# Attention of a hybrid layer: two query blocks score into one two-bank tile, and weighted values, transposes and scores of neighbouring steps form one run on TensorE

## The chip, the cores and the metric

The kernel runs on one core of a Trainium2 chip. The metric is device time in microseconds (us) of one execution; the time of a kernel is the median of its runs. The engines are TensorE (PE, with PEld for its weight loads), VectorE (DVE), ScalarE (ACT), GpSimd (POOL) and SyncE (SP). Each engine takes its own instructions in a fixed order and waits on semaphores.

## The reference

One inference step of one layer: a combined input projection of RMSNorm(x) feeds a convolution branch and a dilated sliding-window attention; both are gated, projected and added; a gated feed-forward with a short convolution follows. 1024 prompt tokens and 8 sample tokens (1032 columns) run together. The change concerns the attention of the prompt:

```python
D_MODEL, SEQ, HEAD_DIM, HEADS_PER_GROUP = 1024, 1024, 64, 4
GROUPS = ((128, 1), (512, 4), (2048, 16))          # window, dilation
...
    s = jnp.einsum('brnqhd,brnkhd->brnhqk', qb, kb).astype(jnp.float32)
    ...
    s = jnp.where(valid[None, None, :, None], s, NEG)
    mx = jnp.max(s, axis=-1, keepdims=True)
    p = jnp.exp(s - mx)
    den = jnp.sum(p, axis=-1, keepdims=True)
    o = jnp.einsum('brnhqk,brnkhd->brnqhd', p, vb.astype(jnp.float32))
    o = o / jnp.swapaxes(den[..., 0], -1, -2)[..., None]
```

After permuting the tokens by the dilation, every group has eight blocks of 128 queries for each head. A block sees its own 128 keys and, where one exists, the 128 before it.

## The kernel before, in words

Attention is done in six units, one for each group g and pair of heads p; unit b = 2g + p. A unit (`attention_unit`, L570) writes three projection jobs, q, k and v, by `in_jobs`: each makes three banks of 344 columns, 24 matmuls to a bank (`product`, matmul at L215; three passes of split operands over eight blocks of depth). ACT evacuates each bank (L553), DVE applies the rotary embedding to q and k (`rope`, L538 to L549). After each bank `mm_blocks` calls `pump` (L125), which takes the next item or items of queues: `later` (one item, and one more for each `LD` = 9 that wait), `second`, `third`, and `taps`, the depthwise convolution (`conv_wide`, L494, one tap of some 1000 columns on DVE at a time, L502). So attention's steps and the taps are written between the banks of projections of the units that follow; after unit 5 the gate projections ga and gb are the cover. A scheduler then gives each engine its fixed order, following what is written, the buffers and its own idea of times; `after` adds an order between two instructions.

The items of a unit are `values` (L589: eight transposes of v, two banks), ten of `step` (L644), the samples' scores, and `store`. `step(t)` weighs block t − 2, turns block t − 1 and scores block t:

- `scores(i)` (L599): for each head a matmul (L612) of 64 rows, 128 queries by 128 or 256 keys, into a one-bank tile of tag "s" (two of them); then a DVE reduction (L613) that adds the mask, writes `sm` and gives the maximum; one negation `nm` (L617) for both heads; two exponentials on ACT (L620) that write `pr` and the denominators. Of the 48 blocks 22 have 256 keys and 26 have 128.
- `turn(i)` (L623): transposes of `pr` on PE (L629; two or four) into a bank of tag "t", evacuated by ACT as `pk` (L631).
- `weigh(i)` (L633): two or four matmuls with the values (L639), into a bank of tag "o", evacuated by ACT into `ot` (L642).

`sm`, `pr` and `pk` have two buffers each. The eight banks of PSUM are given by tag: mm 4, s 2, t 1, o 1. `combine` (L696) later weighs the groups, `layer_norm` (L778) belongs to the convolution branch; both use banks of the same tags.

## Time and profile before

| | before |
|---|---|
| time, median of three runs | 1666.64 us (1660.62 to 1666.67) |
| profiled execution | 1664.54 us, span 1662.8 us |
| PE busy | 1622.7 us, 98% |
| DVE busy | 1125.7 us, 68% |
| ACT busy | 608.1 us, 37% |
| POOL busy | 178.4 us, 11% |
| mean granted clock of PE | 0.993 |

The profile is one execution, taken on the chip. Its span runs from the first to the last instruction. Busy is the union of an engine's instructions; matmuls are pipelined, so that a row lasts longer than the step to the next one. A windows view cuts the span into stretches and gives busy time for each engine; the timeline lists instructions by start; the chain of waits follows the last work back to what released it. The attention stretch is 229 to 570 us.

### The profile page before, as it was taken

Reading aid. Unit: us, or ns where it says so; the run is one execution under the profiler, and the core shown is the slowest. Engines: PE = TensorE matmul, PEld = TensorE weight load, DVE = VectorE, ACT = ScalarE, POOL = GpSimd, SP = SyncE. Lnnn points to the kernel's source line nnn. Section 1 sums busy time; section 2 is a strip of 40 time slices with the busy share of each in tenths; the row PEclk is TensorE's granted clock in tenths of the full one; section 3 lists DMA queues with packets and bytes.
Section 4 is the critical chain, followed back from the end, with each engine's and each line's share of the span. In section 5 each row is a group of like instructions: output and inputs, shape, how many; then the busy total and the mean of one; then the engine's idle time right before and its main releaser. Section 6 shows DMA issues by size and latency. Waiting matters only on the chain.

```text
span 1662.8 us, 26829 instructions
## 1 busy us (share of the span) xinstructions
PE 1622.7 (98%) x11044; PEld 1576.3 (95%) x11044; DVE 1125.7 (68%) x1747; ACT 608.1 (37%) x1079; POOL 178.4 (11%) x269
## 2 busy tenths in 40 slices
PE   8999999999999999999999989999999999999997
PEld 7999998898899999999999989999999998999997
DVE  5889998798986996764435786666666666324246
ACT  6411123344434223452223454444444444221023
POOL 0111011011102102130001001111111110000002
PEclk9999999999999999999999999999999999999999
DMA  8544332232325457893553135655655557752102
GB/s 291 187 129 125 95 118 81 83 94 80 116 92 191 137 171 247 225 355 127 184 195 117 49 115 153 178 153 153 178 153 153 153 128 271 286 197 83 48 26 102
DMA packets 86986, 250.19 MB, mean 150 GB/s; under 512 B 10128, under 2 KB 31664, under 8 KB 86864
## 3 DMA queue, kind: packets, MB, share of 16 engines
q1 hardware_dynamic: 57984, 157.85, 28.6%
q0 software_dynamic: 28880, 90.64, 18.9%
q8 instruction: 86, 1.41, 0.3%
q14 instruction: 36, 0.29, 0.1%
HBM read 201.11 MB, written 92.46 MB: 177 GB/s over the span
## 4 chain that ended last, share of the span: by engine, by line
PE 85%; DMA 7%; DVE 3%; ACT 2%; issue 2%; SPq 0%; POOL 0%; DVEq 0%; POOLq 0%; ACTq 0%
PE dn L215 13%; PE qb L1077 9%; PE ga L215 6%; PE oa L215 5%; PE gb L215 5%; PE xo L215 5%; PE v L215 4%; PE k L215 4%; PE q L215 4%; PE qc L1077 4%; PE al L215 4%; DMA sa<-w_ups 3%; PE ag L215 3%; PE first L215 3%; PE qa L1077 2%; PE s L612 2%
## 5 line engine op out<-in xcount | busy, mean ns | idle before, releaser
L502 DVE SCALAR_TENSOR_TENSOR ca<-cu,c_w_dw,ca 128x1019 f32<-128x1019 f32 (+22 forms) x240 | 300.3, 1268 | 1.7
L215 PE MATMUL dn<-gl,hi_wd 128*128 128x344 f32 x456 | 147.5, 323 | 2.6 <-DVE gl L68 2.6
L215 PE MATMUL dn<-gh,hi_wd 128*128 128x344 f32 x456 | 147.0, 323 | 1.2 <-ACT gh L68 1.2
L215 PE MATMUL dn<-gh,lo_wd 128*128 128x344 f32 x456 | 146.8, 322 | 0.0
L934 DVE TENSOR_TENSOR xs<-dn,xs 128x1032 f32<-128x1032 f32 x26 | 32.0, 1232 | 123.0 <-PE dn L215 115.9
L1057 DVE TENSOR_TENSOR sb<-sa,raw_ra 128x512 f32<-128x512 f32 x20 | 13.8, 692 | 114.7 <-DMA sa<-w_ups 112.9
L215 PEld LDWEIGHTS dn<-gl,hi_wd 128*128 128x128 f32 x456 | 86.6, 190 | 4.4 <-DVE gl L68 4.4
L215 PEld LDWEIGHTS dn<-gh,hi_wd 128*128 128x128 f32 x456 | 86.5, 190 | 1.9 <-ACT gh L68 1.9
L215 PEld LDWEIGHTS dn<-gh,lo_wd 128*128 128x128 f32 x456 | 86.5, 190 | 0.0
L68 ACT ACTIVATE hi_wd<-raw_wd 128x896 fp32r<-128x896 f32 (+1 forms) x24 | 23.7, 987 | 140.7 <-PE dn L215 139.0
L1077 PE MATMUL qb<-t,hi_wc 128*128 128x258 f32 x320 | 60.4, 289 | 7.4 <-ACT s L1128 7.4
L215 PE MATMUL xo<-mh,hi_wo 128*128 128x344 f32 x192 | 62.3, 325 | 3.3 <-DVE xr L960 3.3
L215 PE MATMUL ga<-hh,lo_ga 128*128 128x344 f32 x192 | 62.5, 325 | 0.0
L215 PE MATMUL ga<-hh,hi_ga 128*128 128x344 f32 x192 | 62.4, 325 | 0.0
L215 PE MATMUL ga<-hl,hi_ga 128*128 128x344 f32 x192 | 62.3, 325 | 0.0
L215 PE MATMUL xo<-ml,hi_wo 128*128 128x344 f32 x192 | 62.1, 324 | 0.0
L215 PE MATMUL gb<-hl,hi_gb 128*128 128x344 f32 x192 | 62.0, 323 | 0.0
L215 PE MATMUL xo<-mh,lo_wo 128*128 128x344 f32 x192 | 61.9, 322 | 0.0
L215 PE MATMUL gb<-hh,lo_gb 128*128 128x344 f32 x192 | 61.8, 322 | 0.0
L215 PE MATMUL oa<-sl,hi_wco 128*128 128x344 f32 x192 | 61.5, 320 | 0.0
L215 PE MATMUL oa<-sh,lo_wco 128*128 128x344 f32 x192 | 61.5, 320 | 0.0
L215 PE MATMUL gb<-hh,hi_gb 128*128 128x344 f32 x192 | 61.1, 318 | 0.0
(820 smaller groups left out, 5429.4 us busy)
## 6 DMA issues: line engine op xcount, KB each, us to landing
o_k<-cache_k SPq DMA_DIRECT2D x16, 1023.5 KB, 7.4
o_v<-cache_v SPq DMA_DIRECT2D x16, 1023.5 KB, 7.7
g<-g_dram SPq DMA_DIRECT2D x22, 516.0 KB, 8.2
sa<-w_ups SPq DMA_DIRECT2D x20, 512.0 KB, 3.6
sa<-w_ups POOLq DMA_DIRECT2D x20, 512.0 KB, 5.7
raw_ra<-w_ups SPq DMA_DIRECT2D x20, 512.0 KB, 3.6
raw_wd<-w_down SPq DMA_DIRECT2D x16, 448.0 KB, 3.2
hi_wd<-w_ups POOLq DMA_DIRECT2D x20, 256.0 KB, 3.5
```

The source lines that it names most:

```text
L68: ins = op(*args, **kwargs)
L215: ins = nc.tensor.matmul(ps[:, :m], wk, xk, start=(k == 0 and i == 0), stop=(k == n - 1 and i == 2))
L502: after(anchor[0], nc.vector.scalar_tensor_tensor(acc[:, d:SEQ], u[:, :SEQ - d], w[:, 30 - d:31 - d], acc[:, d:SEQ], ALU.mult, ALU.add))
L612: nc.tensor.matmul(sps[:, :nk], q[hs, i * P:(i + 1) * P], k[hs, k0:k0 + nk], start=True, stop=True)
L934: nc.vector.tensor_tensor(out=v3(t), in0=ps, in1=v3(t), op=ALU.add)
L1057: nc.vector.tensor_tensor(out=s2, in0=s1, in1=ra[:, 512:], op=ALU.add)
L1077: nc.tensor.matmul(ps[:, s, :SUB], wk, xk, start=(first and k == 0 and i == 0), stop=(k == 3 and i == 2), skip_group_check=True)
```

## The change

The score tile of tag "s" becomes one tile of two banks, one bank for each head, with two query blocks side by side in a bank. A step now handles two blocks: a unit has six steps, in which step t weighs double block t − 2, turns t − 1 and scores t. Four score matmuls follow each other, then four reductions, one negation of four maxima, and four exponentials. The second transposed block of a step goes into a bank of tag "mm". Weighted values of both blocks, and the samples' products, share one "o" bank and one evacuation.

`run` and `ready` bind a step on PE. `after(run[0], ...)` holds transposes behind the weighted values of the step and scores behind the transposes. `ready(exps[t], ...)` is a semaphore dependence: the transposes of double block t, and the weighted values of t − 1 that stand before them, wait for the last exponential of t. So the three pieces stand as one run with no projection between. `values` and the transposes in `combine` use the two-bank tile and one evacuation each; the small sums of `layer_norm` take banks of three tags and lose two yields inside loops.

```diff
-PSA = {"mm": 4, "s": 2, "t": 1, "o": 1}
+PSA = {"mm": 4, "s": 1, "t": 1, "o": 1}
...
+    def two_banks(name):
+        return psb[0].tile([P, 2, 512], F32, tag="s", name=name, bufs=1)
...
+    def ready(first, then):
+        tc.add_manual_dep(
+            then.ins, first.ins.name,
+            mybir.DependencyInfo(mybir.DependencyClass.Sync, mybir.DependencyReason.DATA),
+            reason="together",
+        )
...
         def values():
...
+            ps = two_banks(f"vtr{b}")
+            for i in range(8):
+                nc.tensor.transpose(ps[:, i // 4, i % 4 * P:(i % 4 + 1) * P], vt[:, i * P:(i + 1) * P], ident)
+            nc.scalar.activation(v, ps.rearrange("p h (i c) -> p (h i) c", c=P), AF.Copy)
...
+        probs, turned, exps, extra, run = {}, {}, {}, [], [None]
+        def scores(t):
+            sps = two_banks(f"s{b}{t}").rearrange("p h (i k) -> p h i k", i=2)
+            for i in (2 * t, 2 * t + 1):
+                nk, k0, _ = keys(i)
+                for h in range(2):
+                    hs = slice(h * HALF, (h + 1) * HALF)
+                    after(run[0], nc.tensor.matmul(sps[:, h, i % 2, :nk], q[hs, i * P:(i + 1) * P], k[hs, k0:k0 + nk],
+                                                   start=True, stop=True))
+            nm = small.tile([P, 2, 2], F32, tag="nm", name=f"nm{b}{t}")
...
+                for h in range(2):
+                    nc.vector.tensor_tensor_reduce(
+                        out=sms[i][:, h, :nk], in0=sps[:, h, i % 2, :nk], in1=mask, scale=1.0, scalar=-3e38,
+                        op0=ALU.add, op1=ALU.max, accum_out=mx[:, i % 2, h:h + 1])
             anchor[0] = nc.vector.tensor_scalar(nm, mx, -1.0, None, ALU.mult)
...
+                for h in range(2):
+                    exps[t] = nc.scalar.activation(
+                        probs[i][:, h, :nk], sms[i][:, h, :nk], AF.Exp, bias=nm[:, i % 2, h:h + 1],
+                        accum_out=ot[:, i, 2 * HALF + 2 + h:2 * HALF + 3 + h])
+
+        def turn(t):
+            for i, tag in ((2 * t, "t"), (2 * t + 1, "mm")):
...
+                        ins = nc.tensor.transpose(tps[:, o:o + P], probs[i][:, h, kb * P:(kb + 1) * P], ident)
+                        ready(exps[t], ins)
+                        after(run[0], ins)
+                run[0] = ins
...
+        def weigh(t):
+            ops = bank(f"o{b}{t}", "o")
...
+                        run[0] = nc.tensor.matmul(ops[:, c:c + HALF], turned[i][:, o:o + P],
+                                                  v[:, k0 // P + kb, h * HALF:(h + 1) * HALF],
+                                                  start=(kb == 0), stop=(kb == nk // P - 1))
+                        if t + 1 in exps:
+                            ready(exps[t + 1], run[0])
+            for products in extra:
+                products(ops[:2 * NS, 2 * P:3 * P + 1])
+            extra.clear()
+            nc.scalar.activation(ot[:, 2 * t:2 * t + 2, :2 * HALF], ops[:, :2 * P].rearrange("p (i c) -> p i c", i=2),
+                                 AF.Copy)
 
         def step(t):
+
             if 0 <= t - 2:
                 weigh(t - 2)
-            if 0 <= t - 1 < 8:
+            if 0 <= t - 1 < 4:
                 turn(t - 1)
-            if t < 8:
+            if t < 4:
                 scores(t)
...
-        for t in range(10):
+        for t in range(6):
             later.append(lambda t=t: step(t))
-            if t == 1:
-                later.append(lambda: later.insert(3, sample_scores()))
+            if t == 0:
+                later.append(lambda: later.insert(3, lambda products=sample_scores(): extra.append(products)))
...
+        ps = two_banks(f"otr{p}")
+        for i in range(8):
+            nc.tensor.transpose(ps[:, i // 4, i % 4 * P:(i % 4 + 1) * P], os_[0][:, i, :], ident)
+        split(ps.rearrange("p a b -> p (a b)"), oT_h[:, :SEQ], oT_l[:, :SEQ])
+        yield
...
+            ps = bank(f"lm{c}", "sto"[c])
             nc.tensor.matmul(ps[:, :CW], onesm, c_sum[:, cs(c)], start=True, stop=True)
             nc.scalar.activation(mub[:, cs(c)], ps[:, :CW], AF.Copy, scale=1.0 / DM)
-            yield
+        yield
```

The order of the built programs shows what this does at three places. Names end in a running number; s51 is step 1 of unit 5, in the kernel before s521 is block 2, head 1. In the kernel after, the matmul of `product` is L226, scores L618, transposes L647, weighted values L662, reductions L628, the negation L631, taps L513, exponentials L636.

PE, unit 5, before, at block 2:

```order
L612 MATMUL s520_5014<-k5r_4604,q5r_4424 128x128
L612 MATMUL s521_5017<-k5r_4604,q5r_4424 128x128
L639 MATMUL o50_5004<-vk5_4778,pk50_4947 128x64 x2
L629 MATMUL pt51_5008<-c_ident_120,pr51_4958 128x128 x2
L215 MATMUL ga2_1_5233<-hh2_95,lo_ga2_5175 128x344
L215 MATMUL ga2_1_5233<-hh3_96,hi_ga2_5174 128x344
L215 MATMUL ga2_1_5233<-hl3_104,hi_ga2_5174 128x344
```

PE, unit 5, after, at steps 0 to 2:

```order
L618 MATMUL s50_4746<-k5r_4492,q5r_4324 128x128 x4
L647 MATMUL pt50_4801<-c_ident_120,pr50_4759 128x128 x2
L647 MATMUL pt51_4806<-c_ident_120,pr51_4762 128x128 x2
L618 MATMUL s51_4811<-k5r_4492,q5r_4324 128x128 x4
L662 MATMUL o50_4830<-vk5_4638,pk50_4804 128x64 x2
L662 MATMUL o50_4830<-vk5_4638,pk51_4809 128x64 x2
L647 MATMUL pt52_4836<-c_ident_120,pr52_4824 128x128 x2
L647 MATMUL pt53_4841<-c_ident_120,pr53_4827 128x128 x2
L618 MATMUL s52_4846<-k5r_4492,q5r_4324 128x128 x4
```

Before, projections (ga2_1) follow each small group; after, three steps follow one another with no projection between. In other steps of the kernel after, one bank of projections, 24 rows, stands between two such runs (48 at step 3 of a unit).

DVE, unit 0, before, around the reductions of block 3:

```order
L617 TENSOR_SCALAR nm02_2391<-ot0_2193 128x2
L68 TENSOR_TENSOR lo_k2_2858<-raw_k2_2855,hi_k2_2857 128x1024
L540 STREAM_SHUFFLE k1p_2516<-k1t_2195 128x1032
L502 SCALAR_TENSOR_TENSOR ca3_2186<-cu3_2184,c_w_dw_788,ca3_2186 128x1016
L613 ISA sm03_2437,ot0_2193<-s030_2438,c_mask_band_794 128x256
L613 ISA ot0_2193 128x1
L502 SCALAR_TENSOR_TENSOR ca2_1730<-cu2_1728,c_w_dw_788,ca2_1730 128x997
L613 ISA sm03_2437,ot0_2193<-s031_2441,c_mask_band_794 128x256
L613 ISA ot0_2193 128x1
L541 TENSOR_TENSOR k1t_2195<-k1t_2195,rope_c_920 128x1032
```

DVE, unit 0, after, between the negated maximum of step 1 (nm01) and the first reduction of step 2 (sm04):

```order
L68 TENSOR_TENSOR lo_k2_2822<-raw_k2_2819,hi_k2_2821 128x1024
L551 STREAM_SHUFFLE k1p_2491<-k1t_2195 128x1032
L513 SCALAR_TENSOR_TENSOR ca2_1730<-cu2_1728,c_w_dw_788,ca2_1730 128x998
L513 SCALAR_TENSOR_TENSOR ca3_2186<-cu3_2184,c_w_dw_788,ca3_2186 128x1015
L552 TENSOR_TENSOR k1t_2195<-k1t_2195,rope_c_920 128x1032
L553 TENSOR_TENSOR k1p_2491<-k1p_2491,rope_s_921 128x1032
L513 SCALAR_TENSOR_TENSOR ca2_1730<-cu2_1728,c_w_dw_788,ca2_1730 128x997
L513 SCALAR_TENSOR_TENSOR ca3_2186<-cu3_2184,c_w_dw_788,ca3_2186 128x1014
L555 TENSOR_TENSOR k1t_2195<-k1t_2195,k1p_2491 128x1032
L513 SCALAR_TENSOR_TENSOR ca2_1730<-cu2_1728,c_w_dw_788,ca2_1730 128x996
L513 SCALAR_TENSOR_TENSOR ca3_2186<-cu3_2184,c_w_dw_788,ca3_2186 128x1013
L628 ISA sm04_2476,ot0_2193<-s02_2470,c_mask_band_794 128x256
```

Before, the reductions of a block stand among the rope of k1 and the taps; after, the whole rope, the split lo_k2 and six taps come ahead of the first reduction.

ACT, unit 0, before, from the exponentials of block 2 to those of block 4:

```order
L620 ACTIVATE pr02_2393,ot0_2193<-sm02_2384,nm02_2391 128x256 x2
L553 ACTIVATE vt1_2196<-v1_0_2529 128x344
L642 ACTIVATE ot0_2193<-o01_2424 128x128
L631 ACTIVATE pk02_2435<-pt02_2430 128x512
L553 ACTIVATE vt1_2196<-v1_1_2582 128x344
L642 ACTIVATE ot0_2193<-o02_2449 128x128
L620 ACTIVATE pr03_2446,ot0_2193<-sm03_2437,nm03_2444 128x256 x2
L68 ACTIVATE hi_v2_3056<-raw_v2_3054 128x1024
L553 ACTIVATE vt1_2196<-v1_2_2635 128x344
L620 ACTIVATE pr04_2471,ot0_2193<-sm04_2462,nm04_2469 128x256 x2
```

ACT, unit 0, after, from the exponentials of step 1 to those of step 2:

```order
L636 ACTIVATE pr02_2414,ot0_2193<-sm02_2407,nm01_2406 128x256 x2
L636 ACTIVATE pr03_2417,ot0_2193<-sm03_2410,nm01_2406 128x256 x2
L670 ACTIVATE ot0_2193<-o00_2448 128x2x128
L652 ACTIVATE pk02_2461<-pt02_2456 128x512
L652 ACTIVATE pk03_2468<-pt03_2463 128x512
L564 ACTIVATE vt1_2196<-v1_0_2504 128x344
L636 ACTIVATE pr04_2483,ot0_2193<-sm04_2476,nm02_2475 128x256 x2
L636 ACTIVATE pr05_2486,ot0_2193<-sm05_2479,nm02_2475 128x256 x2
```

In the kernel after, the evacuation of v1_0, the bank of projections between the scores s02 and the run that needs pr04 and pr05, stands ahead of the exponentials that write them. The same holds for a bank of the cover at steps 0.1, 1.1, 2.1, 3.1 and 4.1 (unit and step).

## Rows read from the trace of the kernel before

**Rows 1.** The page: each engine's busy us, share of the span, instructions.

```profile
PE 1622.7 (98%) x11044; PEld 1576.3 (95%) x11044; DVE 1125.7 (68%) x1747; ACT 608.1 (37%) x1079; POOL 178.4 (11%) x269
```

**Rows 2.** Windows, all engines: us, PE, PEld, DVE, ACT, POOL busy, PEclk, DMA, GB/s.

```profile
229.00:570.00 341.00, 341.00 (x2202) 307.50 (x2201) 291.86 (x522) 132.05 (x387) 44.57 (x66) 1.00 0.32 103
```

**Rows 3.** The same window, L215 alone: us, PE, PEld, PEclk, DMA, GB/s.

```profile
229.00:570.00 341.00, 258.81 (x1446) 226.74 (x1445) 1.00 0.32 103
```

**Rows 4.** The chain that ended last, one piece: piece and start, us, what.

```profile
105.16 11.33 PE ag L215 x72
```

**Rows 5.** Timeline of PE, one-head score runs of 256 columns: start, us, what.

```profile
330.50 0.32 PE L215 MATMUL v<-hh,lo_v 128*128 128x344 f32 x1
330.75 0.70 PE L612 MATMUL s<-k1t,q1t 64*128 64x256 f32 x2
...
331.73 0.70 PE L612 MATMUL s<-k1t,q1t 64*128 64x256 f32 x2
...
332.62 0.32 PE L215 MATMUL q<-hh,lo_q 128*128 128x344 f32 x1
```

**Rows 6.** Timeline of PE, both heads of a 256 block in one run.

```profile
374.75 0.32 PE L215 MATMUL v<-hl,hi_v 128*128 128x344 f32 x1
375.00 0.70 PE L612 MATMUL s<-k2r,q2r 64*128 64x256 f32 x4
...
375.89 0.32 PE L215 MATMUL v<-hh,hi_v 128*128 128x344 f32 x1
```

**Rows 7.** Timeline of PEld, the weight loads of the first run in rows 5.

```profile
330.74 0.29 PEld L612 LDWEIGHTS s<-k1t,q1t 64*128 64x128 f32 x2 [0.21 <-issue]
```

**Rows 8.** Timeline of PE, both heads of a 128-wide block in one run.

```profile
472.96 0.32 PE L215 MATMUL k<-hh,hi_k 128*128 128x344 f32 x1
473.21 0.49 PE L612 MATMUL s<-k4r,q4r 64*128 64x128 f32 x4
...
473.90 0.32 PE L215 MATMUL k<-hh,lo_k 128*128 128x344 f32 x1
```

**Rows 9.** Timeline of all engines, a quick chain: two reductions, two exponentials.

```profile
398.38 0.42 DVE L613 CUSTOM_DVE_ANT_0 sm<-s,c_mask_band 128x256 f32<-128x256 f32 x1
...
398.72 0.42 DVE L613 CUSTOM_DVE_ANT_0 sm<-s,c_mask_band 128x256 f32<-128x256 f32 x1
...
399.45 0.51 ACT L620 ACTIVATE pr<-sm,nm 128x256 f32<-128x256 f32 x1 [1.36 <-DVE nm L617]
...
399.95 0.49 ACT L620 ACTIVATE pr<-sm,nm 128x256 f32<-128x256 f32 x1
```

**Rows 10.** Timeline of all engines, a slow chain: scores and their negated maximum.

```profile
259.33 0.70 PE L612 MATMUL s<-k0t,q0t 64*128 64x256 f32 x2
...
268.53 0.16 DVE L617 TENSOR_SCALAR nm<-ot 128x2 f32<-128x2 f32 x1
```

**Rows 11.** Groups on DVE, 229 to 570 us: count, busy us, mean ns, idle.

```profile
L502 DVE SCALAR_TENSOR_TENSOR ca<-cu,c_w_dw,ca 128x1006 f32<-128x1006 f32 x5 | 6.3, 1269 | 0.0
...
L68 DVE TENSOR_TENSOR lo_k<-raw_k,hi_k 128x1024 fp32r<-128x1024 f32 x4 | 4.9, 1223 | 0.7 <-ACT hi_k L68 0.7
...
L540 DVE STREAM_SHUFFLE k1p<-k1t 128x1032 f32<-128x1032 f32 x1 | 1.3, 1328 | 0.0
...
L541 DVE TENSOR_TENSOR k1t<-k1t,rope_c 128x1032 f32<-128x1032 f32 x1 | 1.2, 1228 | 0.0
```

**Rows 12.** Groups on ACT, 229 to 570 us, the same columns.

```profile
L620 ACT ACTIVATE pr<-sm,nm 128x256 f32<-128x256 f32 x44 | 22.0, 501 | 17.8 <-DVE nm L617 17.8
L620 ACT ACTIVATE pr<-sm,nm 128x128 f32<-128x128 f32 x52 | 20.3, 394 | 17.0 <-DVE nm L617 14.3 <-DVE cmb L714 2.7
...
L553 ACT ACTIVATE vt<-v 128x344 f32<-128x344 f32 x16 | 7.2, 450 | 5.3 <-PE v L215 5.3
```

**Rows 13.** Windows, all engines, at a gap of PE; columns as in rows 2.

```profile
907.00:911.00 4.00, 0.69 (x6) 0.41 (x4) 4.00 (x11) 3.17 (x8) 0.00 (x0) 0.98 0.14 57
911.00:914.00 3.00, 3.00 (x11) 3.00 (x12) 3.00 (x7) 0.48 (x1) 0.54 (x1) 0.50 0.50 120
```

More of the change, by code (lines that the diff above doesn't have):

```diff
@@ L278, in token_rstd, with spread @@
         return rsqrt(ps, [t[:, i, :ps.shape[-1]] for i in range(3)])
-    def spread(r, name, behind=None, n=CW, d=None):
+    def spread(r, name, behind=None, n=CW, d=None, tag="s"):
         offs = offsets(n)
@@ L290, in spread @@
         )
-        ps = bank(f"sp_{name}", "s")
+        ps = bank(f"sp_{name}", tag)
         for j, off in enumerate(offs):
@@ L599, in keys @@
             return (2 * P if prev else P), ((i - 1) * P if prev else i * P), prev
-        probs, turned = {}, {}
-        def scores(i):
-            nk, k0, prev = keys(i)
-            mask = mask_d if g == 2 else (mask_b if prev else mask_b[:, P:])
-            sm = scratch(f"sm{b}{i}", "sm").rearrange("p (h k) -> p h k", h=2)
-            mx = ot[:, i, 2 * HALF:2 * HALF + 2]
-            den = ot[:, i, 2 * HALF + 2:2 * HALF + 4]
-            for h in range(2):
-                sps = bank(f"s{b}{i}{h}", "s")
-                hs = slice(h * HALF, (h + 1) * HALF)
-                nc.tensor.matmul(sps[:, :nk], q[hs, i * P:(i + 1) * P], k[hs, k0:k0 + nk], start=True, stop=True)
-                nc.vector.tensor_tensor_reduce(
-                    out=sm[:, h, :nk], in0=sps[:, :nk], in1=mask, scale=1.0, scalar=-3e38,
-                    op0=ALU.add, op1=ALU.max, accum_out=mx[:, h:h + 1])
-            nm = small.tile([P, 2], F32, tag="nm", name=f"nm{b}{i}")
-            anchor[0] = nc.vector.tensor_scalar(nm, mx, -1.0, None, ALU.mult)
-            probs[i] = scratch(f"pr{b}{i}", "pr").rearrange("p (h k) -> p h k", h=2)
-            for h in range(2):
-                nc.scalar.activation(probs[i][:, h, :nk], sm[:, h, :nk], AF.Exp, bias=nm[:, h:h + 1],
-                                     accum_out=den[:, h:h + 1])
@@ new lines, in turn @@
+        def turn(t):
+            for i, tag in ((2 * t, "t"), (2 * t + 1, "mm")):
+                nk = keys(i)[0]
+                tps = bank(f"pt{b}{i}", tag)
+                for h in range(2):
+                    for kb in range(nk // P):
+                        o = h * nk + kb * P
+                        ins = nc.tensor.transpose(tps[:, o:o + P], probs[i][:, h, kb * P:(kb + 1) * P], ident)
+                        ready(exps[t], ins)
+                        after(run[0], ins)
+                run[0] = ins
+                turned[i] = scratch(f"pk{b}{i}", "pk")
+                nc.scalar.activation(turned[i][:, :2 * nk], tps[:, :2 * nk], AF.Copy)
@@ new lines, in weigh @@
+        def weigh(t):
+            ops = bank(f"o{b}{t}", "o")
+            for i in (2 * t, 2 * t + 1):
+                nk, k0, _ = keys(i)
+                for h in range(2):
+                    c = i % 2 * P + h * HALF
+                    for kb in range(nk // P):
+                        o = h * nk + kb * P
+                        run[0] = nc.tensor.matmul(ops[:, c:c + HALF], turned[i][:, o:o + P],
[8 more added lines that the diff above has]
+                                 AF.Copy)
@@ L744, in combine @@
             yield
-        for half in range(2):
-            ps = bank(f"otr{p}{half}", "t")
-            for i in range(4):
-                nc.tensor.transpose(ps[:, i * P:(i + 1) * P], os_[0][:, half * 4 + i, :], ident)
-            sl = slice(half * 512, half * 512 + 512)
-            split(ps, oT_h[:, sl], oT_l[:, sl])
-            yield
+        ps = two_banks(f"otr{p}")
[3 more added lines that the diff above has]
+        yield
         third.append(sample_out(p))
@@ L802, in layer_norm @@
         for c in ALL:
-            nc.scalar.activation(rb[:, cs(c)], spread(rl[:, 3 * c:3 * c + 3], f"lv{c}"), AF.Copy)
-            yield
+            nc.scalar.activation(rb[:, cs(c)], spread(rl[:, 3 * c:3 * c + 3], f"lv{c}", tag="sto"[c]), AF.Copy)
+        yield
         for k in range(KB):
```

43 lines of the change are left out of this document (12 added, 31 removed).

## The prediction, made before the changed kernel ran

> **What bounds the kernel now.** I read the page's totals first: TensorE (PE) is busy 98% of the span [rows 1], so the time is PE's work plus PE's holes. Then the windows of the stretch the change touches, 229 to 570 us, from the first scores to the last weighted values: PE is busy in all 341.00 us, at a granted clock of 1.00, the upper of its two levels (2.4 GHz), VectorE (DVE) in 291.86, ScalarE (ACT) in 132.05 [rows 2]. PE never waits there, so before the change every small piece of attention costs its PE time and every chain on DVE and ACT is hidden. How much is attention: 72 projection matmuls of L215 take 11.33 us, 0.157 each [rows 4]; the stretch has 1446 of them [rows 3], 227.5 us. The other 113.5 us are attention's small matmuls.
>
> What hides the chains? Scores wait for nothing, then DVE makes two masked maxima and the negated maximum, ACT two exponentials, and only then PE can transpose. The trace has quick chains (first reduction at 398.38, second exponential at 399.95 [rows 9]) and slow ones: scores at 259.33 have their negated maximum at 268.53 [rows 10], since DVE had taps, rope and a split in hand. Before the change the transposes stand late enough for both: over all 48 blocks they start 2.9 to 8.1 us after their exponentials.
>
> **Part 1, what PE saves.** A score run between two projection matmuls costs a fixed part and a stream part. Two one-head runs of 256 columns with one projection between stretch 330.50 to 332.62 [rows 5]: less three projections of 0.157, 0.82 each. A run with both heads of a block goes from 374.75 to 375.89 less two projections, 0.83 [rows 6]: the second head is free. With 128 columns it is 473.90 − 472.96 − 0.31 = 0.63 [rows 8]. So 128 more columns cost 0.21, a 256 block streams 0.42, and 0.41 is fixed. In the trace 24 runs are like [rows 5] and 10 like [rows 6]; of the 128-wide, 22 are one-head (0.62) and 15 paired (0.63): 71 runs, 19.7 + 8.3 + 13.6 + 9.5 = 51 us. After, there are 24 runs with two blocks each: 24 × 0.41 + 22 × 0.42 + 26 × 0.21 = 24.5. Saving **26.5 us**. If the fixed part is paid again by a run's second block, the 48 blocks cost 22 × 0.83 + 26 × 0.63 = 34.6 and the saving is 16.5: the other bound. I take 26.5, since the second head paid nothing.
>
> The second block loads weights into rows that the first block's matmul still uses. That happens within one head already: two loads take 0.29 us together [rows 7], and both are over while the matmuls of 0.70 [rows 5] run, so the load hid. The Trainium skill, "TensorE: Matmul & The Clock Gate", Part 3, The mechanism, says a weight load overlaps a running matmul when its row group does not conflict. By that rule 48 loads at the pace of [rows 7] would stand bare, some 5 us, and the saving would be 21.4; the row speaks against it here.
>
> Transposes, weighted values and the samples' products keep their number and form, so I give them nothing. Halved evacuations of weighted values and negated maxima, the merged evacuations of `values` and `otr`, and the yields that `layer_norm` loses are on ACT and DVE; PE's cover hides them before, and after 570 us PE still bounds. If that cover fails, they are at most a microsecond each, inside my range. Nothing moves on POOL's or SP's queues but the position of the samples' loads, which land long before use.
>
> **Part 2, what PE now waits for.** The order shows the price of the one run: transposes of step t, and weighted values of step t−1 ahead of them, wait for all four exponentials of step t, and the next scores stand behind. Between a score run and that wait stand 24 projection matmuls (24 × 0.157 = **3.78 us**), 48 at the last step of a unit, other numbers at its first, and none at steps 0 and 1 of the last unit (written 5.0 and 5.1). Queued behind the waiting transposes on PE are the next scores and all later projections.
>
> The chain at its fastest, for two 256 blocks: first scores there at about 0.75 us, four reductions 0.34 apart [rows 9], 0.73 from the last reduction to the first exponential [rows 9], four exponentials of 0.50 [rows 9, 12]: 0.75 + 1.02 + 0.73 + 2.0 = 4.5. PE arrives at 1.25 (0.41 + 2 × 0.42) + 3.78 = 5.0. So on free engines the cover is just enough. Two things in the order make it too little.
>
> (a) *ACT's order.* In steps 0.1, 0.2, 1.1, 2.1, 3.1 and 4.1 the evacuation of the very projections that form the cover stands ahead of the exponentials. It can't start before PE has done them (5.0 plus about 0.25 for the end of the pipeline), takes 0.45 [rows 12], and then come the four exponentials: 2.0, or 1.8 where two are 128 wide. PE waits 2.3 to 2.8 us in each, whatever DVE does: 15.6 together. In 5.0 and 5.1 there is no cover at all: the score run ends at 0.83, the chain of four 128-wide pieces needs over 3.5; 3.5 and 2.8 at least. With small ones at 1.0 and 4.0 the floor is **23 us**.
>
> (b) *DVE's order.* Whole ropes, splits and taps stand ahead of the reductions. The worst is 0.2: between the negated maximum of step 0.1 and the first reduction of 0.2 stand six taps, three passes of rope, a shuffle and a split, 6 × 1.26 + 3 × 1.23 + 1.33 + 1.22 = 13.8 [rows 11], about 13 with the overlap that neighbours show. Four reductions, a tap and the maximum bring it to 16 us. PE needs only 4.4 us from that maximum to the scores of 0.2 (exponentials, run), so the new maximum comes 11 to 11.6 us after them and the last exponential at 13.2 or later; PE arrives at 5.0 and waits **8.3**. The same working for each step gives 0.1: 3.8, 1.0: 0.9, 1.1: 3.9, 2.1: 5.1, 3.1: 5.6, 4.0: 0.9, 4.1: 3.0, 4.2: 0.9, 5.0: 4.1, 5.1: 3.5, and nothing at the other 13. Sum **40 us**, of which (a) is 23. With DVE 10% quicker than its rows it would be 35, with no overlap of neighbours 43.
>
> The Trainium skill, "Perfetto Trace Analysis", Matmuls, says that independent groups should rotate through PSUM banks so that an evacuation overlaps the next group's matmuls; the change goes from two score tiles to one, against it. The order has the next scores behind the waits on the exponentials anyway, so by rows it adds nothing to the sum.
>
> (c) *The clock.* PE idled from 907 to 911 us (0.69 busy of 4.00), and in the next 3 us it was granted 0.50, the lower level (1.2 GHz) [rows 13]: 1.5 us lost. Six or seven of the stalls are as long as that one or longer. At 1.5 each they cost 10 at most; part comes back, since a slower PE gives DVE time and shortens the next stall; the low end is nothing. I take **6**.
>
> **Sum.** The profiled execution took 1664.5 us (span 1662.8 and 1.7 around it), 2 below the median of 1666.64. 1664.5 − 26.5 + 40 + 6 = **1684 us**.
>
> **Rivals.** *A. The run is the gain it looks like*: DVE and ACT have their pieces ready in time, PE never waits: 1664.5 − 26.5 = 1638. For it: the quick chains of [rows 9], and DVE has 49 us free in the stretch [rows 2]. Against it: the evacuations ahead of the exponentials are in the program, and only two steps need to be like [rows 10] for 15 us. *B. Only the floor*: DVE is never behind, because each hole of PE lets it catch up, and the clock stays up: 1664.5 − 26.5 + 23 = 1661, no change that can be measured (with 16.5 saved, 1671). For it: DVE's total does not grow. Against it: 13 us of DVE work in one step can't be caught up in a cover of 3.78. *C. Worse than the forecast*: the second block pays its fixed part again (10 us) and every long stall costs the clock (4 more): 1698. The slower side turns on one thing: whether the wait for the exponentials, priced in (a) and (b), adds up to more than the 26.5 saved; that is decided as soon as DVE delays two steps by 2 us beyond the floor. That the change doesn't do what it says is no rival: the order shows each run unbroken.
>
> **How the numbers follow.** A measurement of this kernel can tell about 0.5%, 8.3 us, from no change: faster is below 1658.3, slower above 1675. Forecast with its own spread (1675 to 1695) 0.58, C 0.12, B 0.21, A and what lies between A and B 0.09. Slower 0.69, same 0.22, faster 0.09. The range takes in B with a little less stall and most of C: 1656 to 1702.
>
> **What would show it.** Right: in the windows of the stretch PE is no longer full, with holes of 8 us before the transposes of step 0.2, 5 to 6 at 2.1 and 3.1, 4 at 5.0, charged to the exponentials (or, in (b), with DVE busy throughout); score runs of about 1.25 us for two 256 blocks; clock at 0.5 after the longest holes. Wrong: PE full in the stretch (A), holes of under 3 us only (B), or score runs of 1.65 (the saving is 16.5). A hole at a place where no exponentials are awaited, as at `values` for the one score tile, would be a wait that I have not priced.

## The result and the profile after

The changed kernel takes 1700.88 us (median of four runs, 1696.17 to 1702.38); the kernel before took 1664.88 us over the four runs beside it. The ratio is 1.0228, with a 95% interval of 1.0207 to 1.0248: slower by 36 us. The forecast was 1684 us with a range of 1656 to 1702. The sign held, the time is at the very end of the range, and the loss against the kernel before is twice the one forecast (36 us instead of 17 to 20).

The profiled execution took 1700.83 us, its span is 1699.0 us, 36.2 longer than before. The page's totals and the windows of the attention stretch answer to [rows 1] and [rows 2] (columns: length, PE, PEld, DVE, ACT, POOL busy, PEclk, DMA share, GB/s):

```profile
PE 1620.5 (95%) x11044; PEld 1588.6 (93%) x11044; DVE 1123.4 (66%) x1721; ACT 605.9 (36%) x1047; POOL 174.0 (10%) x269
```

```profile
229.00:570.00 341.00, 304.95 (x1973) 285.11 (x1971) 266.60 (x467) 121.17 (x340) 38.56 (x60) 0.91 0.28 89
```

Two things are new in this stretch. PE, which was full, is idle for 36 us of the 341. And PEclk, which was 1.00, is 0.91: for part of the time PE was granted its lower level. PE's waits (in us in total, times, longest) name who it waited for:

```profile
PE o L662 <- ACT pr L636: 29.3, 7, 5.6
...
PE pt L647 <- ACT pr L636: 6.7, 3, 4.1
...
PE sp_lv L304 <- DVE diag_lv L68: 2.4, 1, 2.4
```

The first two lines are ten waits for exponentials, 36.0 us, none of which the kernel before had. Seven are at weighted values (L662), which stand first in a run, three at transposes (L647). The third line is the small sum of `layer_norm`, 2.4 us.

The largest wait belongs to step 0.2. The timeline of DVE from the negated maximum of step 0.1 to that of 0.2:

```profile
258.42 0.20 DVE L631 TENSOR_SCALAR nm<-ot 128x4 f32<-128x4 f32 x1
258.49 1.25 DVE L68 TENSOR_TENSOR lo_k<-raw_k,hi_k 128x1024 fp32r<-128x1024 f32 x1
...
259.64 1.33 DVE L551 STREAM_SHUFFLE k1p<-k1t 128x1032 f32<-128x1032 f32 x1
260.83 2.46 DVE L513 SCALAR_TENSOR_TENSOR ca<-cu,c_w_dw,ca 128x998 f32<-128x998 f32 x2
263.17 1.26 DVE L552 TENSOR_TENSOR k1t<-k1t,rope_c 128x1032 f32<-128x1032 f32 x1
264.31 1.27 DVE L553 TENSOR_TENSOR k1p<-k1p,rope_s 128x1032 f32<-128x1032 f32 x1
265.46 2.48 DVE L513 SCALAR_TENSOR_TENSOR ca<-cu,c_w_dw,ca 128x997 f32<-128x997 f32 x2
267.81 1.27 DVE L555 TENSOR_TENSOR k1t<-k1t,k1p 128x1032 f32<-128x1032 f32 x1
268.96 2.47 DVE L513 SCALAR_TENSOR_TENSOR ca<-cu,c_w_dw,ca 128x996 f32<-128x996 f32 x2
271.31 0.46 DVE L628 CUSTOM_DVE_ANT_0 sm<-s,c_mask_band 128x256 f32<-128x256 f32 x1
...
273.85 0.20 DVE L631 TENSOR_SCALAR nm<-ot 128x4 f32<-128x4 f32 x1
```

DVE has no gap in these 15.4 us; 12.9 of them pass before the first reduction, where the prediction had about 13. On PE the scores of this step had started at 265.30, so the reduction found them 6.0 us old:

```profile
265.30 1.41 PE L618 MATMUL s<-k0t,q0t 64*128 64x256 f32 x8
```

```profile
276.28 0.47 PE L662 MATMUL o<-vk,pk 128*128 128x64 f32 x1 [5.59 <-ACT pr L636]
```

Between those two rows lie 24 projections, 11.0 us, of which the last 5.59 are a hole that ends with the exponentials. What follows the hole is the second new thing. Windows right after it, and after the hole of 5.09 us that ends at 385.30 (columns as above):

```profile
276.30:283.00 6.70, 6.70 (x30) 6.15 (x32) 2.87 (x5) 1.58 (x3) 1.37 (x3) 0.50 0.47 160
385.40:392.20 6.80, 6.80 (x31) 5.82 (x32) 1.51 (x8) 1.36 (x3) 0.00 (x0) 0.50 0.00 0
```

PE is busy in all 6.7 or 6.8 us, at 0.50, the lower level (1.2 GHz). Score runs show it directly. Two rows of the same work, a 128 and a 256 block, at step 2.1 (upper level) and at step 2.2 (lower):

```profile
375.25 0.93 PE L618 MATMUL s<-k2r,q2r 64*128 64x128 f32 x8
```

```profile
389.30 1.65 PE L618 MATMUL s<-k2r,q2r 64*128 64x128 f32 x8
```

Taking the trace's periods at 0.50 together: after the holes there are eight in the attention stretch, 3.4 to 13.7 us long, in which PE was busy for 48.9 us and did the work of 24.5. So the lower clock cost **24.5 us** there, and 1.7 more after the wait of `layer_norm`.

### The profile page after: what moved, and what is told of

The parts are those of the page before. It is cut to its first block, busy times and chain, and to the rows that moved or that the text cites. A ratio compares the mean times of both kernels' runs of the same rounds, so it can differ in the third digit from the quotient of the medians.

```text
span 1699.0 us, 26764 instructions
## 1 busy us (share of the span) xinstructions
PE 1620.5 (95%) x11044; PEld 1588.6 (93%) x11044; DVE 1123.4 (66%) x1721; ACT 605.9 (36%) x1047; POOL 174.0 (10%) x269
## 3 DMA queue, kind: packets, MB, share of 16 engines
q1 hardware_dynamic: 57984, 157.85, 27.9%
## 4 chain that ended last, share of the span: by engine, by line
PE 77%; DMA 8%; DVE 7%; issue 4%; ACT 3%; POOL 0%; SPq 0%; DVEq 0%; POOLq 0%; ACTq 0%
PE dn L226 12%; PE qb L1104 9%; PE ga L226 5%; PE oa L226 5%; PE xo L226 5%; PE qc L1104 4%; PE al L226 4%; PE q L226 4%; PE v L226 4%; PE ag L226 3%; PE first L226 3%; DMA sa<-w_ups 3%; PE qa L1104 2%; PE o L662 2%; PE gb L226 2%
## 5 line engine op out<-in xcount | busy, mean ns | idle before, releaser
L513 DVE SCALAR_TENSOR_TENSOR ca<-cu,c_w_dw,ca 128x1023 f32<-128x1023 f32 (+27 forms) x240 | 299.4, 1272 | 1.8
L226 PE MATMUL dn<-gl,hi_wd 128*128 128x344 f32 x456 | 146.4, 321 | 2.9 <-DVE gl L68 2.9
L226 PE MATMUL dn<-gh,hi_wd 128*128 128x344 f32 x456 | 145.7, 320 | 1.8 <-ACT gh L68 1.8
L226 PE MATMUL dn<-gh,lo_wd 128*128 128x344 f32 x456 | 145.7, 319 | 0.0
L226 PEld LDWEIGHTS dn<-gl,hi_wd 128*128 128x128 f32 x456 | 85.6, 188 | 4.6 <-DVE gl L68 4.6
L226 PEld LDWEIGHTS dn<-gh,hi_wd 128*128 128x128 f32 x456 | 85.5, 188 | 2.4 <-ACT gh L68 2.4
L226 PEld LDWEIGHTS dn<-gh,lo_wd 128*128 128x128 f32 x456 | 85.7, 188 | 0.0
L662 PEld LDWEIGHTS o<-vk,pk 128*128 128x128 f32 x280 | 41.2, 227 | 31.7 <-ACT pr L636 31.7
L662 PE MATMUL o<-vk,pk 128*128 128x64 f32 x280 | 42.4, 311 | 29.4 <-ACT pr L636 29.3
L226 PE MATMUL xo<-mh,hi_wo 128*128 128x344 f32 x192 | 62.4, 325 | 4.0 <-DVE xr L987 3.3
L226 PE MATMUL gb<-hl,hi_gb 128*128 128x344 f32 x192 | 62.9, 328 | 0.0
L226 PE MATMUL ga<-hl,hi_ga 128*128 128x344 f32 x192 | 62.5, 326 | 0.0
L226 PE MATMUL ga<-hh,hi_ga 128*128 128x344 f32 x192 | 62.3, 324 | 0.0
L226 PE MATMUL ga<-hh,lo_ga 128*128 128x344 f32 x192 | 62.2, 324 | 0.0
L226 PE MATMUL xo<-ml,hi_wo 128*128 128x344 f32 x192 | 62.2, 324 | 0.0
L226 PE MATMUL gb<-hh,lo_gb 128*128 128x344 f32 x192 | 62.0, 323 | 0.0
L226 PE MATMUL xo<-mh,lo_wo 128*128 128x344 f32 x192 | 61.9, 322 | 0.0
L226 PE MATMUL oa<-sl,hi_wco 128*128 128x344 f32 x192 | 61.4, 320 | 0.0
```

Source lines behind the costliest of these rows:

```text
L226: ins = nc.tensor.matmul(ps[:, :m], wk, xk, start=(k == 0 and i == 0), stop=(k == n - 1 and i == 2))
L513: after(anchor[0], nc.vector.scalar_tensor_tensor(acc[:, d:SEQ], u[:, :SEQ - d], w[:, 30 - d:31 - d], acc[:, d:SEQ], ALU.mult, ALU.add))
L662: run[0] = nc.tensor.matmul(ops[:, c:c + HALF], turned[i][:, o:o + P], v[:, k0 // P + kb, h * HALF:(h + 1) * HALF], start=(kb == 0), stop= ...
```

## Where the 36 us are

For each profiled execution I take three numbers from its trace: PE's idle time between its first and its last matmul, half of PE's busy time at 0.50 (what the lower clock cost), and the span. What is left over I call the saving of the score runs. For the change: 36.2 = 38.5 (more idle) + 22.5 (more loss to the clock) − saving, so the saving is **24.8 us**. The kernel before had 28.4 us idle and lost 7.2 to the clock, all outside the stretch. As a remainder the saving takes up whatever else changed. It comes out between 21 and 28 wherever two blocks are scored in a run, and the score runs priced one by one give some 26; so there is room for a third cause of some 5 us at most. In the table idle and clock are those of the stretch from 225 to 615 us, in us; times are medians, the other three columns are from one profiled execution each.

| kernel | time, median | ratio to before, 95% | PE idle | lost to the clock | saving, from the sum |
|---|---|---|---|---|---|
| before | 1664.88 | | 0 | 0 | |
| after | 1700.88 | 1.0228 (1.0207 to 1.0248) | 36.0 | 24.5 | 24.8 |
| fill_stalls | 1685.45 | 1.0131 (1.0114 to 1.0148) | 10.6 | 3.4 | 24.5 |
| values_free | 1686.12 | 1.0133 (1.0113 to 1.0153) | 28.0 | 16.0 | 26.8 |
| scores_free | 1680.56 | 1.0099 (1.0080 to 1.0118) | 25.7 | 18.1 | 23.6 |
| transposes_free | 1703.31 | 1.0251 (1.0233 to 1.0268) | 41.5 | 23.9 | 26.4 |
| unbound | 1663.77 | 1.0003 (0.9992 to 1.0014) | 12.1 | 6.2 | 21.4 |
| unbound_inplace | 1660.26 | 0.9988 (0.9976 to 0.9999) | 10.3 | 8.4 | 21.1 |
| late_bound | 1657.67 | 0.9966 (0.9955 to 0.9976) | 13.2 | 6.1 | 27.1 |
| late_unbound | 1646.24 | 0.9908 (0.9883 to 0.9933) | 3.8 | 0.0 | 26.9 |
| heads_only | 1660.62 | 0.9984 (0.9971 to 0.9997) | 0.0 | 0.0 | 10.9 |
| short_taps | 1672.99 (one run) | | 20.0 | 18.7 | 27.9 |

## The experiments

### Is it the clock? PE kept busy in the holes

```diff
+        def fill(bank_tile, n):
+            for _ in range(n):
+                ins = nc.tensor.matmul(bank_tile[:, 400:512], ident, ident[:, :112], start=True, stop=True)
+                after(last_mm[0], ins)
+                after(last_s[0], ins)
+                after(run[0], ins)
+                run[0] = ins
...
             ops = bank(f"o{b}{t}", "o")
+            fill(ops, FILL.get((b, t + 1), 0))
```

> The kernel after, with idle matmuls (identity by 112 columns of the identity, written to columns of PSUM that nobody reads) put at eight places between the end of the cover and the run that waits for the exponentials: 18, 22, 10, 20, 22, 12, 16 and 12 of them at steps 0.1, 0.2, 1.1, 2.1, 3.1, 4.1, 5.0 and 5.1, sized to take a little less than the measured waits. The chains on DVE and ACT and the order of all else stay. Theory (the missing 24 us are the lower clock that follows a long hole): the granted clock stays at 1.00 in the whole stretch, score runs of two 256 blocks take 1.25 instead of up to 2.08 us, the time from each score run to its transposes stays as it is (9.5, 11, 9, 10 us), and the time falls by 20 to 24 us, to 1677 to 1681. Rival (the score runs save less than 26.5 us, or matmuls after a wait are slow for another reason): the time stays at 1697 to 1702, or grows by what the added matmuls take beyond the waits.

Measured: 1685.45 us, ratio 1.0131. 15.4 us go, less than the 20 to 24 expected. The clock does nearly what the theory says. The windows of the stretch show 0.99, not 1.00: two periods of 3.4 us at 0.50 are left, after the two longest holes that remain, 1.89 and 1.86 us. PE's idle time is down to 10.6 us:

```profile
229.00:600.00 371.00, 360.44 (x2527) 342.50 (x2526) 308.36 (x515) 131.13 (x361) 49.26 (x72) 0.99 0.32 101
```

The added matmuls took 30.8 us (groups of PE by shape; busy us, mean ns of one record):

```profile
L617 PE MATMUL o<-c_ident 128*128 128x112 f32 x232 | 27.0, 275 | 0.0
...
L617 PE MATMUL pt<-c_ident 128*128 128x112 f32 x32 | 3.8, 278 | 0.0
```

Each filling starts in the pipelined end of the matmul before it, 1.1 us in all. Without the filling matmuls PE would count 40.3 us of idle time in the stretch, against 36.0 in the kernel after. So a PE that is quicker between the holes stands 4.3 us longer in them, as the chains have not become quicker by as much: 21.1 us less lost to the clock, 4.3 given back as waiting. That makes 16.8; 15.4 were measured, with another 1 us of clock and holes outside the stretch. The clock's net share of the slowdown is thus some 15 us, and the rival (score runs that save less) falls: 24.5 us of saving are in this run too. One thing did not stay as expected: at step 0.2 the order of DVE has one tap fewer ahead of the negated maximum, which comes 14.3 us after that of step 0.1 instead of 15.4.

### Is it DVE's queue? Short taps

```diff
             after(anchor[0], nc.vector.scalar_tensor_tensor(
-                acc[:, d:SEQ], u[:, :SEQ - d], w[:, 30 - d:31 - d], acc[:, d:SEQ], ALU.mult, ALU.add))
+                acc[:, d:d + 64], u[:, :64], w[:, 30 - d:31 - d], acc[:, d:d + 64], ALU.mult, ALU.add))
```

> The kernel after, where each of the convolution's 240 taps on DVE works on 64 columns instead of some 1000 (so most of the convolution is left out). DVE is then far from full. Theory (DVE's queue, not the binding by itself, sets how long PE waits): the negated maximum comes within 4 us of each score run, only what ACT's order forces is left, 2.3 to 2.8 us a step at 0.1, 0.2, 1.1, 2.1, 3.1, 4.1 and about 3 at 5.0 and 5.1, 20 us in all instead of 36, and the lower clock costs half of its 24 us: time 1700.9 - 16 - 12 = 1673, a few us less where other stages waited for DVE. Rival (the chain itself is too long for 24 projections): the waits keep at 30 us or more and the time at 1690 or more.

Measured: 1672.99 us in a single run, where 1673 was expected. That the total agrees is luck: the waits fell by 16 us as expected, the clock's loss by 6 instead of 12, and another 6 us came from outside the stretch and from a larger saving. The waits fell from 36.0 to 20.0 us, near the 23 that step (a) of the prediction has for a DVE that is never behind. Six of its eight waits are 2.4 to 3.1 us long:

```profile
PE o L662 <- ACT pr L636: 14.6, 5, 3.1
```

At steps 0.1 and 1.1, where step (a) has 2.3 to 2.8 us "whatever DVE does", PE didn't wait at all. ACT's order differs there from the kernel after: the four exponentials stand ahead of the evacuation. At step 0.1, the last exponential and the evacuation:

```profile
253.78 0.49 ACT L636 ACTIVATE pr<-sm,nm 128x256 f32<-128x256 f32 x1
...
255.22 0.43 ACT L564 ACTIVATE k1t<-k 128x344 f32<-128x344 f32 x1
```

So short taps changed two things at these steps, DVE's queue and ACT's order. At 0.2, 2.1, 3.1 and 4.1 the waits of (a) stayed, 2.4 to 3.1 us each. The clock still cost 18.7 us, not the 12 expected: a hole of 2.41 us at 364.68 was followed by 6.8 us at 0.50 just as one of 5.09 was in the kernel after. So with most of DVE's work out of the way the change would still not pay: 27.9 us saved stand against 20.0 waited and 18.7 lost to the clock.

### Which part of the binding? One part taken off at a time

```diff
-                    after(run[0], nc.tensor.matmul(sps[:, h, i % 2, :nk], q[hs, i * P:(i + 1) * P], k[hs, k0:k0 + nk],
-                                                   start=True, stop=True))
+                    nc.tensor.matmul(sps[:, h, i % 2, :nk], q[hs, i * P:(i + 1) * P], k[hs, k0:k0 + nk],
+                                 start=True, stop=True)
```

> The kernel after with one part of the binding taken off: scores are no longer held behind the transposes of their step. Transposes and weighted values still wait for all four exponentials. In its order the scores of step t + 1 then stand ahead of the run that waits for the exponentials of step t. Theory (what costs most is that a late chain holds back the start of the next one): each run gets one more score run of about 1.1 us as cover, and the next chain's scores are there before the wait, not after it: the waits fall from 36 to 12 to 20 us, the clock's loss from 24 to about 10, time 1664.5 - 25 + 16 + 10 = 1666, 1658 to 1674. Rival (it is the wait for four exponentials that costs, wherever the scores stand): waits of 30 us, time 1690 to 1700.

Measured: 1680.56 us, ratio 1.0099. This is a miss for both sides: waits of 25.7 us, neither 12 to 20 nor 30. Each run got one score run as cover, but with the scores out of the way the waits stay, for weighted values and transposes still stand before four exponentials:

```profile
PE o L662 <- ACT pr L636: 21.1, 8, 4.3
```

```diff
-                        if t + 1 in exps:
-                            ready(exps[t + 1], run[0])
```

> The kernel after with the other part taken off: weighted values no longer wait for the exponentials of the next step. Scores still stand behind the transposes, and these wait for all four exponentials. The order on PE stays nearly the same. Theory: weighted values (0.9 to 1.8 us a step, seven of the eight long waits) move into the hole ahead of the transposes and the chain stays as long as it was: the waits fall by 9 to 11 us to about 26, the clock still drops after each, time 1700.9 - 10 - 3 = 1688, 1683 to 1694. Rival (weighted values' wait is the binding that matters): waits under 15 us and time under 1675.

Measured: 1686.12 us, ratio 1.0133; 1688 was expected. The waits move from weighted values to transposes and shrink to 28.0 us, by the weighted values that now run in the hole:

```profile
PE pt L647 <- ACT pr L636: 27.6, 11, 4.8
```

```diff
-                        ready(exps[t], ins)
                         after(run[0], ins)
```

> The kernel after with the third part of the binding taken off: transposes wait only for the exponential whose output they read, no longer for all four. Weighted values still wait for all four of the next step, scores still stand behind the transposes. Theory: at seven of the eight long waits the weighted values stand first and wait as before, so only step 5.0 and the two small waits at 1.0 and 4.0 shorten, 1.5 to 3 us in all: 1697 to 1701. Rival (it is the transposes' wait that matters): waits fall by 10 us or more, time under 1690.

Measured: 1703.31 us, ratio 1.0251, 2 us above the expected 1697 to 1701. The expected small gain didn't come. In five of the six units the order now has 12 to 20 projections of the first bank of cover ahead of the scores of step 1, between the pieces of the transposes, and only 4 to 12 are left behind these scores as cover. At step 0.1 that makes the longest hole before a run in any of the kernels, with 7 projections behind the scores:

```profile
254.71 1.13 PE L618 MATMUL s<-k0t,q0t 64*128 64x256 f32 x8
...
266.36 0.47 PE L661 MATMUL o<-vk,pk 128*128 128x64 f32 x1 [9.22 <-ACT pr L636]
```

In the profiled execution a looser wait made PE wait longer (41.5 us idle against 36.0), because cover went to a place where nothing was waited for. In the medians the difference to the kernel after, 2 us, is within the intervals.

All three taken off together:

> The kernel after without the binding on PE: no dependence of transposes and weighted values on all four exponentials, no order that holds scores behind the transposes. The two-bank score tile and the steps of two blocks stay. Theory (the binding makes the waits): in its order the next scores stand ahead of the transposes in most steps and 20 projections between the transposes' pieces, so each wait is 1 to 3 us shorter: 15 to 20 us in all instead of 36, the clock costs 8 to 12 instead of 24, time 1664.5 - 25 + 17 + 10 = 1667, 1660 to 1675. Rival (steps of two blocks with one score tile make the waits, bound or not): waits of 30 us or more stay, time 1690 or more.

Measured: 1663.77 us, ratio 1.0003 (0.9992 to 1.0014), expected 1667. The waits are 12.1 us, the clock costs 6.2. So the binding as a whole is worth 37 us; taken off alone, its three parts are worth 20, 15 and nothing that can be told from noise. No single one is the whole cause: with any one part off 25.7 to 41.5 us of idle time remain, with all three off 12.1. Pairs of parts were not tried. The unbound kernel saves 21.4 us in its score runs and smaller pieces and gives 18 of it back in the stretch.

### More cover: transposes one pump step later

```diff
-            if 0 <= t - 2:
-                weigh(t - 2)
-            if 0 <= t - 1 < 4:
-                turn(t - 1)
+            if 0 <= t - 3:
+                weigh(t - 3)
+            if 0 <= t - 2 < 4:
+                turn(t - 2)
...
-                probs[i] = scratch(f"pr{b}{i}", "pr").rearrange("p (h k) -> p h k", h=2)
+                probs[i] = sms[i]
```

(with seven steps to a unit, and four buffers of one tag for what were `sm` and `pr`)

> The kernel after with transposes one pump step later: step t scores t, turns t - 2 and weighs t - 3, seven steps to a unit; the binding into one run stays. So that blocks can wait longer, the exponentials are written in place and the buffers of sm and pr are one tag of four. Theory (what is missing is cover: 24 projections, 3.78 us, against chains of 8 to 11 us): 45 or more projections stand between most score runs and their transposes, waits of 1.5 us at most are left at steps 2.1 and 3.1 and under 1 at 5.1, about 5 in all, the clock stays up, time 1664.5 - 25 + 5 + 3 = 1648, 1642 to 1655, faster than before. Rival (the run itself is the fault, because scores behind it start the next chain too late, or one score tile is too few): the waits move to the scores or stay with the transposes, 20 us or more, time 1670 or more.

Measured: 1657.67 us, ratio 0.9966 (0.9955 to 0.9976): faster than before by 5.6 us, not by the 16 expected. Waits of 13.2 us are left instead of 5, and 6.1 us of clock instead of 3. The largest, 3.4 us, is at step 0.1, which the expectation does not name:

```profile
PE o L663 <- ACT sm L637: 9.8, 6, 3.4
```

More cover takes away two thirds of the waits while every part of the binding stays. The expected 45 projections and more between scores and transposes stand at 16 of the 24 steps. The largest waits left, 3.4 us at 0.1, 2.4 at 4.1 and 2.2 at 5.1, are where the trace has fewer of them: 32, 24 and none. That fits cover against chain as what decides, with the binding lengthening the chain and taking from the cover. This run also gives the blocks other buffers; what these do alone is told below, without the binding.

Both together, the later step and no binding:

> The late transposes of late_bound, and the binding taken off as in unbound: two-bank score tile, steps of two blocks, transposes one pump step later, exponentials in place, no wait on all four exponentials. Theory (waits are cover against chain, and the binding adds to the chain the last two exponentials and the scores that stand behind): waits of late_bound (13 us in the stretch) fall to 5 to 9, the clock's loss from 6 to about 3; but weighted values, transposes and scores stand in more and shorter runs, as in unbound, where the saving came to some 21 us instead of 25 to 27. Time 1664.5 - 23 + 7 + 3 = 1651, 1646 to 1657. Rival (the waits that late_bound has left are set by the two-block steps alone): the waits stay at 12 us or more, and the time at 1657 to 1662.

Measured: 1646.24 us (1640.14 to 1656.27), ratio 0.9908 (0.9883 to 0.9933), 16.4 us faster than the kernel before and the best here. In the stretch PE is idle for 3.8 us and the clock stays up:

```profile
229.00:615.00 386.00, 382.23 (x2613) 365.17 (x2612) 348.48 (x581) 145.57 (x388) 57.91 (x91) 1.00 0.41 130
```

```profile
PE pt L648 <- ACT sm L637: 2.6, 3, 1.1
```

The fear that the saving would shrink to 23 with shorter runs didn't come true: it is 26.9, with all 24 score runs unbroken (unbound has 26). Its profiled execution, the fastest of six, took 1640 us, close to the 1638 of the prediction's rival A, which asked what the two-block scores would give if nothing were late; the median is 6 us above it, for a reason that the profile doesn't show.

To part the two things that late_unbound has over unbound:

> unbound with the exponentials written in place, so that sm and pr share four buffers as in late_unbound, but with the transposes at their old step: it parts the two things that late_unbound has over unbound. Theory (lateness is what counts, 24 more projections between scores and transposes): the order has 24 projections or fewer in most places as in unbound, waits stay at 8 to 13 us, time 1658 to 1666. Rival (buffers are what counts): waits of 5 us or less and a time of 1644 to 1652.

Measured: 1660.26 us, ratio 0.9988 (0.9976 to 0.9999), waits of 10.3 us. The shared buffers alone give 3.5 us, hardly more than the intervals of the two ratios; the later step, on top of them, gives the other 14.

### The pairing of heads alone, in the kernel before

```diff
+            sps = two_banks(f"s{b}{i}")
             for h in range(2):
-                sps = bank(f"s{b}{i}{h}", "s")
                 hs = slice(h * HALF, (h + 1) * HALF)
-                nc.tensor.matmul(sps[:, :nk], q[hs, i * P:(i + 1) * P], k[hs, k0:k0 + nk], start=True, stop=True)
+                nc.tensor.matmul(sps[:, h, :nk], q[hs, i * P:(i + 1) * P], k[hs, k0:k0 + nk], start=True, stop=True)
```

> The kernel before with one part of the change alone: both heads of one block score into one two-bank tile, four banks mm, one such tile, no binding, steps of one block as before (layer_norm's small sums take banks of three tags as in the change). Theory (each score run costs a fixed 0.41 us, and the second head is free): 48 runs instead of 71, 22 x 0.83 + 26 x 0.63 = 34.6 instead of 51 us, 16.5 us saved; with one tile instead of two some scores wait for the reductions of the block before, 0 to 6 us. Time 1664.5 - 16.5 + 3 = 1651, 1647 to 1656. Rival (one score tile for two is what costs, since scores must wait for DVE): waits at the scores of 15 us or more and a time of 1664 or more.

Measured: 1660.62 us, ratio 0.9984 (0.9971 to 0.9997), a gain of 2 us instead of 13. The stretch itself does well, PE is full at the upper level:

```profile
229.00:570.00 341.00, 341.00 (x2273) 313.56 (x2272) 295.63 (x524) 134.15 (x390) 46.98 (x72) 1.00 0.36 109
```

So one score tile for two makes no wait at steps of one block, and the rival falls. But the saving is 10.9 us, not 16.5: nothing in this kernel holds the heads together, and the scheduler still put projections between them in 7 of 48 blocks. The trace has 55 score runs; 14 of them one-head runs, where the kernel before had 46. Merging 6 blocks of 256 and 10 of 128 at 0.81 and 0.61 each makes 11.0, which is what was measured. Later, a wait of 3.9 us at the attention's output projection (L218, tile ob, for DVE) and 2.8 us of the lower clock took part of it back. The profiled execution, 1656.73 us, is among the fastest of the twelve; why the median is another 4 us slower the profile doesn't show.

## Why the prediction came out as it did

**Bound and mechanism: right.** PE was full before, and the change made it wait for the exponentials in the places and for the reason given: DVE's rope, split and taps in front of the reductions, evacuations ahead of the exponentials, 24 projections as cover. Of the sum 1664.5 − 26.5 + 40 + 6, the saving and the waits together are 2 us off; the term that was mis-sized is the clock's.

**The saving: right.** 26.5 us forecast, 24.8 measured. The score runs cost what was worked out: in late_unbound, measured from the projection before to the second one after, less two projections, a run of a 128 and a 256 block takes 1.05 us, of two 256 blocks 1.26, of two 128 blocks 0.84, where 1.04, 1.25 and 0.83 were forecast from [rows 5], [rows 6] and [rows 8]. The first of them, at step 2.3 of late_unbound (364.77 − 363.41 − 0.31):

```profile
363.41 0.32 PE L227 MATMUL v<-hh,hi_v 128*128 128x344 f32 x1
363.66 0.93 PE L619 MATMUL s<-k2r,q2r 64*128 64x128 f32 x8
364.51 0.42 PE L227 MATMUL v<-hl,hi_v 128*128 128x344 f32 x1
364.77 0.32 PE L227 MATMUL v<-hh,lo_v 128*128 128x344 f32 x1
```

The second block pays no fixed part, and its weight loads don't show in the time. So the rule of the Trainium skill ("TensorE: Matmul & The Clock Gate", Part 3, The mechanism) would have priced the run too high: with two bare loads at the pace of [rows 7] the 256 pair would be 1.46, and 1.26 was measured.

**The waits: right, 10% too large.** 40 us forecast, 36.0 measured:

| step | 0.1 | 0.2 | 1.0 | 1.1 | 2.1 | 3.1 | 4.0 | 4.1 | 4.2 | 5.0 | 5.1 |
|---|---|---|---|---|---|---|---|---|---|---|---|
| forecast | 3.8 | 8.3 | 0.9 | 3.9 | 5.1 | 5.6 | 0.9 | 3.0 | 0.9 | 4.1 | 3.5 |
| measured | 4.45 | 5.59 | 1.87 | 2.51 | 5.09 | 5.46 | 0.75 | 3.11 | 0 | 4.06 | 3.09 |

The sum is better than its parts: single steps are off by up to 2.7 us, both ways. The largest miss, 0.2, has two reasons. PE ran at the lower level after the hole of 0.1, so the scores of 0.2 came 6.9 us after the maximum of 0.1, where 4.4 was forecast; and DVE took 15.4 us from maximum to maximum, not 16. So the new maximum came 8.6 us after the scores instead of 11 to 11.6. In the filled kernel, where the clock stayed up until then, PE stood 6.8 us there, still not 8.3, and 40.3 us in all, near the 40 of the forecast.

**The clock: this step failed.** Step (c) put 1.5 us on a long hole, took 6 us in all and 10 at most. It measured 24.5. The 1.5 us were read from a window of 3 us in [rows 13]. The period behind it lasted 3.4 us and cost 1.6, so the window hid little; what failed is that this one period was taken as the price of every hole. The kernel before had two more such periods, 6.8 us each, in which PE was busy for 3.7 and 6.4 us and lost half of that, 1.8 and 3.2:

```profile
910.80:914.20 3.40, 3.25 (x11) 3.25 (x12) 3.40 (x9) 0.49 (x1) 0.54 (x1) 0.50 0.52 119
982.50:989.30 6.80, 3.67 (x17) 3.67 (x18) 6.00 (x8) 4.12 (x5) 1.33 (x2) 0.50 0.24 41
1392.10:1398.90 6.80, 6.44 (x22) 5.56 (x22) 5.07 (x7) 3.34 (x3) 0.00 (x0) 0.50 0.81 281
```

The largest of the three at eight holes would have put the upper bound at 26 instead of 10. In the kernel after the lower level lasted 6.8 or 10.2 us after most of the long holes and 13.7 after the two of unit 5, and PE was busy through most of it. Per period the loss was 1.7 to 5.2 us, 3.1 in the mean. I had also charged it to holes of 3.3 us or more alone; in the kernel after the holes of 1.87 and 2.51 us were followed by 3.4 us at 0.50 each. Some of it does come back, 4.3 us by the filled kernel, but the 36.0 us of waits hold that already. The halving itself was right in (c). The Trainium skill, "TensorE: Matmul & The Clock Gate", HAM oscillation — how this bites in real kernels, prices the lower level in the same way, at half of the time that a kernel is throttled. By that rule the 48.9 busy us at 0.50 cost 24.5; the filled kernel agrees within 1.4 us (16.8 us less by the sum, 15.4 measured).

**What was not priced:** `layer_norm`'s small sums. I gave the yields nothing, and a microsecond at most if PE's cover failed, because PE has other work after 570 us. One wait of 2.4 us (L304) with 1.7 us of clock after it stands there in the kernel after, and one of 3.2 us in values_free. The kernel before and heads_only, which keep the yields, have no such wait; the yields alone were not tested.

**The rivals.** C, at 1698, is what happened in size, but not for its reason: 10 of its 14 us over the forecast were a second fixed part in the score runs, which does not exist. B's floor of 23 us is near what short_taps, with DVE nearly out of the way, waited: 20.0, though not at all of its places. A is what the fastest execution of late_unbound comes near.

## What to carry to other kernels

A run on a full engine that is made shorter by binding steps together needs its inputs earlier by as much as the binding takes away in cover: count, for each place, the work that stands between a producer chain's start and its consumer, and compare it with the slowest chain in the trace, queue of the producing engine included. A hole on PE is to be priced together with the period at the lower clock behind it, read to its end; here that added two thirds to the holes' own length. Fewer, longer score runs saved their 27 us in the profiled execution once the transposes stood one step later and nothing tied the step together; by the medians the kernel was 16 us faster.

## What was not expected of the hardware

The periods at the lower clock were longer than the holes in front of them: 1.87 us of hole at 314.64 in the kernel after was followed by 3.4 us at 0.50, 2.41 us at 364.68 in short_taps by 6.8. Matmuls that nobody reads, put into the holes, kept the clock at 0.99 and made the kernel 15.4 us faster, though they were 30.8 us of extra work on the busiest engine.
